# Stage one of a hybrid encoder: input fed by columns, row sums from matmuls, a fixed order of the first round

## The chip, the cores and the metric

The kernel runs on one core of a Trainium2 chip. The metric is the time of one execution on the device in microseconds (us); a profiled execution also leaves a trace of what each engine did. Engines are named as in the profile: PE (TensorE), DVE (VectorE), ACT (ScalarE), POOL (GpSimd) and SP (SyncE, which here only issues DMAs).

## The reference

One encoder layer is computed for two request groups that share all weights: a sample of 2048 tokens and a prompt of 512 tokens, each 1024 wide.

```
mod = silu(c) @ w_ada + b_ada            # shift, scale, gate_res: one row per group
h = rms_norm(x, g_norm) * (1 + scale) + shift
proj = h @ w_in                          # qa ka va za | cq ckv kr zb | gm
ya = windowed_gqa(qa, ka, va, sink) * silu(za)
yb = mla(cq, ckv, kr, g_q, w_uq, g_kv, w_ukv) * silu(zb)
ga, gb = split(sigmoid(gm))
x + gate_res * ((ga * (ya @ w_oa) + gb * (yb @ w_ob)) @ w_out)   # then a final rms_norm
```

`rms_norm` divides each row (token) by the root of the mean of its squares. The change touches how `h` is made from `x`.

## The kernel before

Everything is float32. A product in full precision is made of three matmuls on a high and a low part of each operand (`mm3`, L99 to L102): the high part is the value rounded by a copy on ACT, the low part is what the rounding left, from a subtraction on DVE (activations) or POOL (weights, L122 and L123).

The 2560 tokens go in five chunks of 512, four of the sample and one of the prompt. Three stages follow each other. Stage one (up to about 520 us) makes `h` and every projection that the latent attention needs. Stage two (to about 1640 us) is the latent attention, in an order written by hand. Stage three makes the gates, the windowed attention and the output.

In stage one the projections want `h` with the 1024 columns on the partitions, in eight tiles of 128 columns by 512 tokens. The input lies by rows. `load_x` (L233) loads four tiles of 128 rows, sums the squares of each row on ACT (L240), raises the mean to the power -1/2 on POOL (L97) and scales the rows on DVE (L242). `x_cols` (L249) turns them: four PE transposes of 128x128 for each of the eight tiles into a PSUM bank (L252). `h_tile` (L255) then makes `h32 = a*x + b` on DVE (L258) and the high part `hh` on ACT (L261), both from the bank and beside each other, and the low part on DVE (L262); `h32` goes to DRAM (`h_d`, L263), where stages two and three fetch it again (`load_h`, L637 and L638).

The columns `a` and `b` (`acol`, `bcol`) come from the modulation, in the block from L516, in four groups of 256 columns: matmuls `pm` (L561) on weights `wa` that stream in, four small copies into `mod` by DVE and ACT in turn (L568, L570), two small matmuls `pc` (L573), and five small DVE steps (L577 to L581). Round a of chunk 0 (`tka`, L100 to L102) multiplies `h` tile by tile into four PSUM banks, one for each 128 tokens, so it follows the four groups. After it come `ka` (one bank, 24 matmuls), round b (`tkb`) and four `qa`, with the tiles of the next chunk made between the `qa`. `norm_c` (L428) ends a bank: a sum of squares on ACT (L432), then a copy to `cn` and a scaling on DVE (L434, L435).

PSUM has four banks for accumulation here, so `ka` can start only when the first bank of round a has been read out. Each engine works through its own queue in order. A scheduler sets that order from its own estimate of times; only stage two is written by hand. Loads of the chunks' weights are issued by ACT, those of input by SP, whose queue they share with the stores of results.

## Time and profile before

| | us |
|---|---|
| median of 3 runs | 2647.18 |
| lowest and highest | 2646.66 and 2648.54 |
| profiled execution | 2646.29 |
| its span, first to last instruction | 2644.5 |
| PE busy in the span | 2563.1 (97%) |
| POOL busy | 1599.2 |
| DVE busy | 1698.1 |
| ACT busy | 1326.4 |

The mean granted clock of TensorE is 0.992 of full speed. A busy engine counts from the start to the end of its instructions, and neighbouring matmuls overlap, so the cost of one is read from the distance of the starts.

### The profile page before, as it was taken

What the parts mean: (1) busy time and instruction counts of PE and PEld (TensorE: products, weight loads), DVE (VectorE), ACT (ScalarE), POOL (GpSimd) and SP (SyncE); (2) the same over time, 40 slices, a digit from 0 to 9 for tenths busy, and PEclk for the clock granted to TensorE, in tenths of its full rate; (3) what the DMA queues carried; (4) which work ended last, traced back from release to release, by engine and by line L of the source; (5) the groups of instructions that cost most, each with busy time, mean ns of one, the idle gap of its engine ahead of it and who ended that gap; (6) DMA issues with size and microseconds to landing.
All of it is one profiled execution on the core that took longest, in us unless ns stands there. A gap on an engine that the chain in (4) does not pass through costs nothing. (4 is left out here: it accounts for less than half of the span.)

```text
span 2644.5 us, 33977 instructions
## 1 busy us (share of the span) xinstructions
PE 2563.1 (97%) x11842; PEld 2036.0 (77%) x11842; DVE 1698.1 (64%) x2511; ACT 1326.4 (50%) x2105; POOL 1599.2 (60%) x992
## 2 busy tenths in 40 slices
PE   6999999899999999999999999999999999999998
PEld 4888888677777777776777777877887788778876
DVE  4654644579999999999864566436644664466325
ACT  3554543267777777777644443434343444344432
POOL 2564554278888888887852376337733773377355
PEclk9999999999999999999999999999999999999999
DMA  8677765563132222212264545344544453445341
GB/s 308 215 241 239 243 208 187 153 185 94 54 95 75 67 79 74 81 58 82 84 218 150 162 167 191 122 148 173 189 133 144 164 193 121 161 152 200 102 172 50
DMA packets 199432, 392.34 MB, mean 148 GB/s; under 512 B 18087, under 2 KB 97384, under 8 KB 197659
## 3 DMA queue, kind: packets, MB, share of 16 engines
q1 hardware_dynamic: 186210, 353.32, 41.3%
q10 hardware_dynamic: 13050, 36.86, 4.3%
q8 instruction: 93, 1.52, 0.2%
q14 instruction: 79, 0.64, 0.1%
HBM read 286.52 MB, written 103.58 MB: 148 GB/s over the span
## 5 line engine op out<-in xcount | busy, mean ns | idle before, releaser
L735 POOL TENSOR_TENSOR pl<-pf,ph 128x1024 fp32r<-128x1024 f32 x272 | 655.6, 2413 | 137.5 <-ACT pf L728 133.9
L123 POOL TENSOR_TENSOR wlgm<-wrgm,whgm 128x1024 fp32r<-128x1024 f32 x80 | 196.5, 2460 | 328.2 <-ACT whgm L122 291.0
L727 ACT ACTIVATE ph<-s 128x1024 fp32r<-128x1024 f32 x272 | 278.7, 1025 | 183.9 <-PE s L720 182.7
L686 DVE TENSOR_REDUCE mx<-mp 128x1 f32<-128x1024 f32 x240 | 292.7, 1220 | 39.0 <-PE mp L680 36.5
L748 DVE TENSOR_TENSOR ac<-ac,pf 128x512 f32<-128x512 f32 x424 | 294.2, 694 | 16.5 <-ACT pf L728 9.6
L728 ACT ACTIVATE pf<-s 128x1024 f32<-128x1024 f32 x272 | 275.8, 1014 | 0.0
L101 PE MATMUL gm<-H,wlgm 128*128 128x512 f32 x640 | 252.3, 395 | 0.0
L100 PE MATMUL gm<-H,whgm 128*128 128x512 f32 x640 | 250.3, 395 | 0.9 <-ACT whgm L122 0.9
L102 PE MATMUL gm<-H,whgm 128*128 128x512 f32 x640 | 251.0, 394 | 0.0
L718 PE MATMUL s<-Q,K 97*128 97x512 f32 x544 | 216.7, 398 | 3.9 <-DMA Q<-qr_d 3.9
L719 PE MATMUL s<-Q,K 96*128 96x512 f32 x544 | 216.9, 399 | 0.0
L720 PE MATMUL s<-Q,K 96*128 96x512 f32 x544 | 215.5, 396 | 0.0
L760 PE MATMUL a<-ph,V 128*128 128x512 f32 x544 | 175.3, 403 | 0.0
L763 PE MATMUL a<-pl,V 128*64 128x512 f32 x544 | 170.7, 395 | 0.9 <-POOL pl L735 0.8
L680 PE MATMUL mp<-K,Q 96*128 96x512 f32 x512 | 162.4, 398 | 5.8 <-DVE mx L686 3.7
L123 POOL TENSOR_TENSOR wlz<-wrz,whz 128x1024 fp32r<-128x1024 f32 x39 | 94.2, 2424 | 120.5 <-ACT whz L122 118.0
L167 DVE CUSTOM_DVE_ANT_0 S<-as,mask,snk 128x384 f32<-128x384 f32 (+1 forms) x160 | 89.2, 585 | 99.2 <-PE as L165 66.9
L188 DVE TENSOR_TENSOR PT<-pT,PT 128x512 fp32r<-128x512 f32 x112 | 77.1, 688 | 108.9 <-ACT PT L187 107.4
L100 PEld LDWEIGHTS gm<-H,whgm 128*128 128x128 f32 x640 | 119.4, 188 | 26.4 <-issue 1.7
L102 PEld LDWEIGHTS gm<-H,whgm 128*128 128x128 f32 x640 | 120.3, 188 | 23.8
L101 PEld LDWEIGHTS gm<-H,wlgm 128*128 128x128 f32 x640 | 120.3, 188 | 23.8
L100 PE MATMUL z<-H,whz 128*128 128x512 f32 x320 | 127.2, 398 | 9.2 <-ACT whz L122 4.8
(254 smaller groups left out, 6501.2 us busy)
## 6 DMA issues: line engine op xcount, KB each, us to landing
wrgm<-in_t_col_dram SPq DMA_DIRECT2D x80, 512.0 KB
wrz<-in_t_col_dram SPq DMA_DIRECT2D x40, 512.0 KB
wrw<-in_t_out_dram SPq DMA_DIRECT2D x40, 512.0 KB
wrqa<-in_t_col_dram ACTq DMA_DIRECT2D x20, 512.0 KB
qa_d<-qa SPq DMA_DIRECT2D x40, 256.0 KB
k_d<-kn SPq DMA_DIRECT2D x20, 512.0 KB
qn_d<-qn SPq DMA_DIRECT2D x20, 512.0 KB
v_d<-vt SPq DMA_DIRECT2D x20, 512.0 KB
```

Source lines behind the costliest of these rows:

```text
L100: nc.tensor.matmul(ps, wh, mh, start=first, stop=False)
L101: nc.tensor.matmul(ps, wl, mh, start=False, stop=False)
L102: nc.tensor.matmul(ps, wh, ml, start=False, stop=last)
L123: (eng or nc.gpsimd).tensor_tensor(out=wl[:, :n], in0=wr[:, :n], in1=f(wh[:, :n]), op=ALU.subtract)
L686: nc.vector.tensor_reduce(out=it.mx[:, i // 2, i % 2:i % 2 + 1], in_=it.mp.rearrange("p a b -> p (a b)"), axis=AX.X, op=ALU.max)
L718: nc.tensor.matmul(ps[:, j, :], K[0:97, 0, ks], Q[0:97, 0, :], start=True, stop=False)
L719: nc.tensor.matmul(ps[:, j, :], K[0:96, 1, ks], Q[0:96, 0, :], start=False, stop=False)
L720: nc.tensor.matmul(ps[:, j, :], K[0:96, 0, ks], Q[0:96, 1, :], start=False, stop=True)
L727: nc.scalar.activation(ph, it.s, AF.Exp)
L728: nc.scalar.activation(pf, it.s, AF.Exp)
L735: nc.gpsimd.tensor_tensor(out=pl, in0=it.pf[p], in1=f(it.ph[p]), op=ALU.subtract)
L748: nc.vector.tensor_tensor(out=sm if last and j else it.acc, in0=it.acc, in1=pf[:, j], op=ALU.add)
```

## The change

The host lays out a copy of the input by columns, in a new DRAM tensor `t_x`. Each chunk loads it with four DMAs of 512 KB (`xT`). The rows are no longer turned. For chunks 1 to 4 the rows are still loaded, but only to sum their squares. `spread` turns the four columns of row factors into one tile `R` in which every partition holds the factors of the 512 tokens: four transposes of a broadcast column, and one ACT copy. Chunk 0 does not load rows at all: `first_x` squares the column tiles on ACT and DVE and sums them over partitions with 32 matmuls against a column of ones.

`h_tile` now makes `h32 = xT*a*R` on DVE, then `hh = h32 + b` on ACT, which follows the DVE step, then the low part on DVE. The tile stored in DRAM lacks `b`, and `load_h` adds it. In `norm_c` the sum of squares writes into `cn` itself, so the DVE copy into `cn` follows it.

In chunk 0, the order on PE is written out: the first modulation group, the spread, and then for each pair of tiles the round's matmuls, with the next modulation group between the two. All weights of round a are loaded by SP between the modulation's weights.

```diff
+        def spread(c, rss):
+            pt = px(tt(c, 0), f"pt{c}")
+            for t in range(4):
+                nc.tensor.transpose(pt[:, t * P:(t + 1) * P], rss[t].broadcast_to([P, P]), ident)
+            R = tl("R", [P, T], F32, f"R{c}", 1)
+            nc.scalar.copy(R, pt)
+            return R
...
-                nc.scalar.activation(jk, xt, AF.Square, accum_out=ss)
+                nc.scalar.activation(xt, xt, AF.Square, accum_out=ss)
                 rstd(rs, ss, D, p1, f"x{c}_{t}", "rvx")
-                nc.vector.tensor_scalar(out=xt, in0=xt, scalar1=rs, scalar2=None, op0=ALU.mult)
-                xts.append(xt)
-            return xts
+                rss.append(rs)
+            return load_xT(c), spread(c, rss)
...
+        def first_x(tp):
...
+                if k % 2:
+                    nc.vector.tensor_tensor(out=sq[:, 1], in0=x, in1=x, op=ALU.mult)
+                else:
+                    nc.scalar.activation(sq[:, 0], x, AF.Square)
+                for t in range(4):
+                    nc.tensor.matmul(pss[t][:, 0:1], sq[:, k % 2, t * P:(t + 1) * P], one, start=(k == 0),
+                                     stop=(k == KD - 1))
...
-            nc.vector.tensor_scalar(out=h32, in0=src, scalar1=acol[:, g, k:k + 1], scalar2=bcol[:, g, k:k + 1],
-                                    op0=ALU.mult, op1=ALU.add)
...
-            nc.scalar.activation(hh[:, 0, :], src, AF.Identity, bias=bcol[:, g, k:k + 1], scale=acol[:, g, k:k + 1])
-            nc.vector.tensor_tensor(out=hh[:, 1, :], in0=h32, in1=f(hh[:, 0, :]), op=ALU.subtract)
+            nc.vector.scalar_tensor_tensor(out=h32, in0=xts[k // 2][:, k % 2], scalar=a, in1=R, op0=ALU.mult,
+                                           op1=ALU.mult)
+            nc.scalar.activation(hh[:, 0, :], h32, AF.Identity, bias=b)
+            nc.vector.scalar_tensor_tensor(out=hh[:, 1, :], in0=h32, scalar=b, in1=f(hh[:, 0, :]), op0=ALU.add,
+                                           op1=ALU.subtract)
...
-                nc.scalar.activation(jk[:, 0:n], ps, AF.Square, accum_out=ss)
+                nc.scalar.activation(dst, ps, AF.Square, accum_out=ss)
...
+            with tc.manual_schedule(engines={nc.tensor.engine}):
+                mod_mm(0)
+                wa_load(3)
+                src0 = src0[0], spread(0, src0[1])
+                mod_fin(0)
+                pss0 = [pa(f"tka0_{t}") for t in range(4)]
+                for q in range(4):
+                    a_mm(2 * q, range(4))
+                    if q == 0:
+                        a_load(3)
+                    if q < 3:
+                        mod_mm(q + 1)
+                        a_split(q + 1)
+                    a_mm(2 * q + 1, range(2))
+                    if q < 3:
+                        mod_fin(q + 1)
+                    a_mm(2 * q + 1, range(2, 4))
...
-        nc.scalar.copy(hh[:, 0, :], hr)
-        nc.vector.tensor_tensor(out=hh[:, 1, :], in0=hr, in1=f(hh[:, 0, :]), op=ALU.subtract)
+        b = bcol[:, c // NS, k:k + 1]
+        nc.scalar.activation(hh[:, 0, :], hr, AF.Identity, bias=b)
+        nc.vector.scalar_tensor_tensor(out=hh[:, 1, :], in0=hr, scalar=b, in1=f(hh[:, 0, :]), op0=ALU.add,
+                                       op1=ALU.subtract)
```

Where PE stands at the end of chunk 0's round a, before: the last of its matmuls (`tka0_3`, on the eighth tile `hh0_7`), and `ka0` behind it.

```order
L101 MATMUL tka0_3_498<-wha0_6_587,hh0_7_474 128x512
L102 MATMUL tka0_3_498<-wla0_6_588,hh0_7_474 128x512
L100 MATMUL ka0_661<-hh0_0_320,whka0_664 128x512
L101 MATMUL ka0_661<-hh0_0_320,wlka0_665 128x512
L102 MATMUL ka0_661<-hh0_0_320,whka0_664 128x512
```

The same place after: three of the four transposes of chunk 1's row factors (`rs1_0` to `rs1_2`) stand between the two.

```order
L101 MATMUL tka0_3_346<-wha0_6_520,hh0_7_545 128x512
L102 MATMUL tka0_3_346<-wla0_6_521,hh0_7_545 128x512
L243 MATMUL pt1_718<-ident_60,rs1_0_681 128x128
L243 MATMUL pt1_718<-ident_60,rs1_1_689 128x128
L243 MATMUL pt1_718<-ident_60,rs1_2_697 128x128
L100 MATMUL ka0_640<-hh0_0_333,whka0_643 128x512
L101 MATMUL ka0_640<-hh0_0_333,wlka0_644 128x512
L102 MATMUL ka0_640<-hh0_0_333,whka0_643 128x512
```

What moved: `ka0` now has three instructions ahead of it that wait for the rows of chunk 1.

SP's queue at that time, before: the stores of chunk 0's `h` (`h_d0`) and the loads of the rows of chunk 1 (`x1`).

```order
L263 DMA h_d0_0_70<-h2_0_318 128x512 x2
L263 DMA h_d0_1_71<-h2_1_369 128x512 x2
L263 DMA h_d0_2_72<-h2_2_418 128x512 x2
L236 DMA x1_0_699<-in_x_sample_dram 128x1024
L236 DMA x1_1_709<-in_x_sample_dram 128x1024
L263 DMA h_d0_3_73<-h2_3_467 128x512 x2
L236 DMA x1_2_719<-in_x_sample_dram 128x1024
L236 DMA x1_3_729<-in_x_sample_dram 128x1024
```

The same after, with chunk 1's columns (`xT1`) behind the rows.

```order
L298 DMA h_d0_0_70<-h2_0_332 128x512 x2
L298 DMA h_d0_1_71<-h2_1_401 128x512 x2
L298 DMA h_d0_2_72<-h2_2_470 128x512 x2
L298 DMA h_d0_3_73<-h2_3_539 128x512 x2
L252 DMA x1_0_678<-in_x_sample_dram 128x1024
L252 DMA x1_1_686<-in_x_sample_dram 128x1024
L252 DMA x1_2_694<-in_x_sample_dram 128x1024
L252 DMA x1_3_702<-in_x_sample_dram 128x1024
L236 DMA xT1_0_710<-in_t_x_dram 128x1024
L236 DMA xT1_1_712<-in_t_x_dram 128x1024
L236 DMA xT1_2_714<-in_t_x_dram 128x1024
L236 DMA xT1_3_716<-in_t_x_dram 128x1024
```

What moved: all stores of chunk 0's `h` stand ahead of the first row load.

PE between the third and the fourth `qa` of chunk 0, before: eight transposes (`pt1_4` and `pt1_5`) of chunk 1's rows.

```order
L101 MATMUL qa0_2_1087<-hh0_7_474,wlqa0_2_1091 128x512
L102 MATMUL qa0_2_1087<-hh0_7_474,whqa0_2_1090 128x512
L252 MATMUL pt1_4_1125<-ident_60,x1_0_699 128x128
L252 MATMUL pt1_4_1125<-ident_60,x1_1_709 128x128
L252 MATMUL pt1_4_1125<-ident_60,x1_2_719 128x128
L252 MATMUL pt1_4_1125<-ident_60,x1_3_729 128x128
L252 MATMUL pt1_5_1136<-ident_60,x1_0_699 128x128
L252 MATMUL pt1_5_1136<-ident_60,x1_1_709 128x128
L252 MATMUL pt1_5_1136<-ident_60,x1_2_719 128x128
L252 MATMUL pt1_5_1136<-ident_60,x1_3_729 128x128
L100 MATMUL qa0_3_1147<-hh0_0_320,whqa0_3_1150 128x512
L101 MATMUL qa0_3_1147<-hh0_0_320,wlqa0_3_1151 128x512
```

The same place after.

```order
L101 MATMUL qa0_2_1049<-hh0_7_545,wlqa0_2_1053 128x512
L102 MATMUL qa0_2_1049<-hh0_7_545,whqa0_2_1052 128x512
L101 MATMUL qa0_3_1099<-hh0_0_333,wlqa0_3_1103 128x512
L102 MATMUL qa0_3_1099<-hh0_0_333,whqa0_3_1102 128x512
L100 MATMUL qa0_3_1099<-hh0_1_338,whqa0_3_1102 128x512
```

What moved: the transposes are gone, and nothing took their place; the transposes of the other six tiles are gone in the same way.

## Rows read from the trace of the kernel before

**Rows 1.** Windows of 66 us: from:to, length, busy us per engine, PEclk, DMA, GB/s

```profile
132.20:198.30 66.10, 66.03 (x362) 57.04 (x361) 38.54 (x69) 35.47 (x74) 43.44 (x70) 1.00 0.76 241
...
330.50:396.60 66.10, 66.10 (x362) 57.47 (x362) 31.54 (x56) 27.07 (x57) 34.64 (x53) 1.00 0.66 208
396.60:420.00 23.40, 21.25 (x104) 16.98 (x103) 8.56 (x13) 8.35 (x16) 6.78 (x12) 0.93 0.33 93
```

**Rows 2.** Timeline, TensorE in chunk 2: start, length us, line, work

```profile
275.69 0.39 PE L102 MATMUL qa<-hh,whqa 128*128 128x512 f32 x1
275.91 0.39 PE L100 MATMUL qa<-hh,whqa 128*128 128x512 f32 x1
276.14 0.60 PE L252 MATMUL pt<-ident,x 128*128 128x128 f32 x4
276.50 0.48 PE L101 MATMUL qa<-hh,wlqa 128*128 128x512 f32 x1
276.81 0.40 PE L102 MATMUL qa<-hh,whqa 128*128 128x512 f32 x1
277.05 0.40 PE L100 MATMUL qa<-hh,whqa 128*128 128x512 f32 x1
```

**Rows 3.** Windows of 10 us while the first projection round runs

```profile
40.00:50.00 10.00, 8.33 (x55) 5.55 (x54) 4.63 (x13) 4.80 (x8) 4.69 (x2) 0.83 0.40 119
50.00:60.00 10.00, 7.15 (x27) 5.48 (x27) 4.56 (x12) 2.43 (x3) 2.10 (x2) 0.78 0.60 206
```

**Rows 4.** Timeline, TensorE in chunk 0, waits in brackets

```profile
26.47 1.19 PE L100 MATMUL tka<-wha,hh 128*128 128x512 f32 x4 [2.84 <-ACT hh L261]
...
41.19 1.48 PE L561 MATMUL pm<-wa,cols 128*2 128x256 f32 x24
42.60 0.61 PE L573 MATMUL pc<-fold,mod 98*128 98x4 f32 x4
...
58.13 0.63 PE L101 MATMUL tka<-wha,hh 128*128 128x512 f32 x1
...
64.04 0.39 PE L102 MATMUL tka<-wla,hh 128*128 128x512 f32 x1
65.09 0.47 PE L100 MATMUL ka<-hh,whka 128*128 128x512 f32 x1 [0.67 <-DVE cn L434]
```

**Rows 5.** Timeline, all engines, copies of the modulation sums

```profile
39.28 0.41 DVE L570 COPY mod<-pm 2x256 f32<-2x256 f32 x1 [3.17 <-PE pm L561]
...
40.59 0.37 ACT L568 COPY mod<-pm 2x256 f32<-2x256 f32 x1 [0.49 <-DVE mod L570]
```

**Rows 6.** Timeline, VectorE of chunk 0, third and fourth modulation group

```profile
44.85 0.98 DVE L258 TENSOR_SCALAR h<-xT,acol,bcol 128x512 f32<-128x512 f32 x2
...
53.09 0.16 DVE L577 TENSOR_TENSOR bcol<-pc,cols 128x2 f32<-128x2 f32 x1 [5.61 <-PE pc L573]
...
53.57 2.77 DVE L258 TENSOR_SCALAR h<-xT,acol,bcol 128x512 f32<-128x512 f32 x2
```

**Rows 7.** Timeline, GpSimd beside it

```profile
53.56 2.04 POOL L123 TENSOR_TENSOR wlb<-wrb,whb 128x864 fp32r<-128x864 f32 x1 [3.50 <-ACT whb L122]
```

**Rows 8.** Groups of VectorE instructions by shape, 60 to 530 us

```profile
L262 DVE TENSOR_TENSOR hh<-h,hh 128x512 fp32r<-128x512 f32 x32 | 35.5, 1113 | 4.8 <-ACT hh L261 4.2
...
L434 DVE COPY cn<-tka 128x384 f32<-128x384 f32 x20 | 10.8, 546 | 0.0
```

**Rows 9.** Groups of ScalarE instructions by shape, 60 to 530 us

```profile
L261 ACT ACTIVATE hh<-pt,bcol,acol 128x512 fp32r<-128x512 f32 x32 | 24.7, 780 | 17.7 <-DVE h L258 17.5
...
L240 ACT ACTIVATE jx<-x 128x1024 bf16<-128x1024 f32 x16 | 16.8, 1053 | 3.2 <-POOL wla L123 3.1
...
L432 ACT ACTIVATE jkcq<-tka 128x384 bf16<-128x384 f32 x20 | 10.0, 499 | 1.6 <-DVE v_cq L96 1.2
```

**Rows 10.** One line, ScalarE reading the hidden tiles back, stages 2 and 3

```profile
L637 ACT CAST H<-hr x40: 603/618/622, 1193.8 to 2362.9; 128x512 fp32r<-128x512 f32 x40
```

**Rows 11.** One line, VectorE on the same tiles: ns min/median/max

```profile
L638 DVE TENSOR_TENSOR H<-hr,H x40: 678/692/2900, 1196.9 to 2363.6; 128x512 fp32r<-128x512 f32 x40
```

More of the change, by code (lines that the diff above doesn't have):

```diff
@@ L230, in rope, with load_xT @@
             nc.gpsimd.tensor_tensor(out=dst[:, :, hi], in0=dst[:, :, hi], in1=tmp[:, :nh, hi], op=ALU.add)
+        def load_xT(c):
+            out = []
+            for k2 in range(KD // 2):
+                xt = tl("hh", [P, 2, T], F32, f"xT{c}_{k2}", NH)
+                nc.sync.dma_start(xt.rearrange("p k n -> p (k n)"), t_x[c, k2])
+                out.append(xt)
+            return out
+        def spread(c, rss):
[5 more added lines that the diff above has]
+            return R
         def load_x(c):
-            xts = []
+            rss = []
             for t in range(4):
@@ L446, in tail_a @@
                 norm_c(t, ps[:, 128:512], 384, cns[t][:, 0:384], "cq")
-            round_("a", [(0, 2), (2, 2), (4, 2), (6, 2)], 512, t_a, tail_a)
+            if c:
+                round_("a", [(0, 2), (2, 2), (4, 2), (6, 2)], 512, t_a, tail_a)
+            else:
+                for t in range(4):
+                    tail_a(t, env["pss0"][t])
             if c == NC - 1:
@@ L487, in chunk @@
                 if nxt is not None:
-                    nH += [h_tile(nxt, k, x_cols(nxts, nxt, k)) for k in (2 * j, 2 * j + 1)]
+                    nH += [h_tile(nxt, k, nxts) for k in (2 * j, 2 * j + 1)]
             C = []
@@ L534, in encoder @@
             sc = cols[:, 0:16].rearrange("p (g k) -> p k g", g=2)
-            XT = []
-            for k in range(KD):
-                if k % 2 == 0:
-                    xt2 = tl("hh", [P, 2, T], F32, f"xT{k}", NH)
-                pt = x_cols(xts, 0, k)
-                if k % 2:
-                    nc.scalar.copy(xt2[:, 1], pt)
-                else:
-                    nc.vector.tensor_copy(xt2[:, 0], pt)
-                XT.append(xt2[:, k % 2])
+            src0 = first_x(p0)
             H = []
@@ L560, in encoder @@
                             r = 32 * (2 * i + n)
[L561 to L564 removed]
+                            nc.tensor.matmul(pm[r:r + 2, 0:256], sc[:, k + i, :], was[q, k][:, i, n, :],
+                                             start=(k == 0), stop=(k == KD - 2))
                 for i in range(4):
@@ L1100 @@
     feeds += list(_tables().items())
+    feeds.append(("t_x", _columns(inputs["x_sample"], inputs["x_prompt"])))
     for name, a in feeds:
```

66 lines of the change are left out of this document (47 added, 19 removed).

## The prediction

> **What bounds the kernel now.** I read the windows first, because a busy share over the whole span hides that the stages differ. From 66 to 396 us PE has no idle time to speak of: the window from 132.2 is busy for 66.03 of 66.10 us, the one from 330.5 for all of it, and the three others between 66 and 396 us look the same; the granted clock is 1.00 [rows 1]. DVE, ACT and POOL are busy for half to two thirds of these windows, and the DMA engines for 0.66 to 0.76. What leaves PE's queue there shortens the run one for one; what is added to another engine is hidden as long as nothing is handed to PE later than now. Two stretches are different. From 396.6 to 420 us PE is busy for 21.25 of 23.40 us at a clock of 0.93 [rows 1]: the last tiles of `h` for the fifth chunk are made there, and PE waits for them. And in the first 65 us a chain runs from engine to engine, round a starting at 26.47 us and ending at 64.43 [rows 4], with the clock at 0.83 and 0.78 in the windows from 40 and from 50 [rows 3]. Stage two keeps its hand-written order, and stage three's matmuls stay the same ones.
>
> **Transposes, chunks 1 to 4.** Of 128 transposes 16 remain (the spread), so 112 go. Their price is a distance, not a duration: from the matmul that starts at 275.91 to the one at 277.05 there lie 1.14 us, for three matmul distances and four transposes. Matmuls start 0.22 to 0.24 apart beside it, 0.23 in the mean, so four transposes cost 1.14 - 0.69 = 0.45, and one 0.113 [rows 2]. 112 x 0.113 = 12.7 us. The DVE scaling of the rows goes too, and the tile's DVE step now reads SBUF in place of a bank: both off PE's path.
>
> **The end of chunk 3.** There the new `h` tiles need no PE and no bank of their own. Only `R` and the loaded columns are needed, both there long before. PE's 2.15 us of idle time in that window should go, and part of the loss to the clock (0.07 x 23.4 = 1.6). I take 3.0; nothing is the other end.
>
> **Chunk 0, until `ka`.** The written order makes the round a period. It begins with 12 matmuls, 12 x 0.227 = 2.7 us (the distance in [rows 2]); then comes a modulation group: 32 matmul records, 24 of which took 1.48, so 2.0 in all [rows 4]. Then PE depends on a chain: the four copies into `mod`, from 39.28 to 40.59 + 0.37, 1.7 us [rows 5]; `pc`, 0.6 [rows 4]; the column steps, from 53.09 to 53.57, 0.5 [rows 6]; two `h32` steps and one low part on DVE, 3 x 0.69, priced by a DVE step with the same two SBUF inputs [rows 11]. The sum is 4.9, with hand-overs 5.0. The remaining 12 matmuls and `pc` lie in that chain's shadow. Period: 2.7 + 2.0 + 5.0 = 9.7 us. The first matmul of the round started at 26.47. The row factors now have to pass the spread and a copy, while eight transposed copies go; I put its start at 27.5. The round would end at 27.5 + 3 x 9.7 + 2 x 2.7 = 62.0 us. To that I add 2.5 for what the ideal chain leaves out: part of the time at half clock (matmuls 0.43 apart, as from 58.13 on, where one lasts 0.63 instead of 0.39 [rows 4]), and POOL beside DVE (below). So the round ends at 64.5, about where it did.
>
> Behind it `ka` now waits longer. Before, it started 0.66 us after the end, once a bank had been read out [rows 4]. In the queue now three transposes of chunk 1's row factors stand ahead of it, and the third row tile is squared on ACT only after the copies of the finished banks, ahead of the square that frees the first bank; the copy to `cn` follows that square instead of running beside it. That is a square of 1.05, a square of 0.50 [rows 9], a copy of 0.55 [rows 8], and about 0.8 for accumulator reads, `va` and hand-overs: 2.9 us. Chunk 1's rows are also loaded later, behind all stores of chunk 0; their DMAs are issued at about 55 us, so the third tile should lie there shortly before 62 and is not what comes last, though closely. `ka` starts at 64.5 + 2.9 = 67.4 instead of 65.09: a loss of 2.3 us. The ends are a gain of 2.4 (62.0 + 0.7) and a loss of 25 (the third rival).
>
> **Stages two and three.** Reading `h` back costs ACT an addition with a bias column instead of a cast. The nearest rows are 0.780 for such a step (from a bank) against 0.618 [rows 9, 10]. Forty times 0.16 is 6.5 us on ACT, hidden under matmuls except for the first tiles of a chunk, where PE waits for the first: two for each of five chunks, 1.6 us. If none is hidden it is 6.5; nothing is the other end. The DVE step keeps its two inputs. The later release of a bank in `norm_c`, 40 times up to 0.55 [rows 8], lies beside other banks' matmuls; I count 1.0 for all, between nothing and 5. The order of stage three also shifts a little in the queues. No row prices that; it can go either way, and I leave it at nothing, plus or minus 3.
>
> **Sum.** -12.7 - 3.0 + 2.3 + 1.6 + 1.0 = -10.8 us against the profiled execution's 2646.29 us, that is 2635.5; the median lies 0.9 above it, so I say 2636.4. The DMA traffic grows by 2 MB a chunk, against some 16 MB in each 66 us (241 GB/s [rows 1]); with a share of 0.76 there is room, and I count nothing. If an in-order queue holds a store behind such a load, a bank comes free later.
>
> **Rivals.**
>
> First, the early stretch gains too. In its favour: in the old order round a shared PE with the tail of the modulation as the scheduler happened to put it, and two of its four weight loads waited in ACT's queue. Then the round ends at 62.0, `ka` starts at 62.7 (-2.4), and the small charges vanish: -12.7 - 3.0 - 2.4 = -18.1, or 2629. Against it: the chain per group has become longer, since ACT's high part now follows DVE.
>
> Second, DVE and POOL get in each other's way, and the gain is mostly lost. A pair of `h32` steps took 0.98 us at 44.85 and 2.77 at 53.57, when a POOL subtraction of 2.04 us started at 53.56 [rows 6, 7]; and the low parts, which read two SBUF tiles, took 1.113 us each in stage one [rows 8] against 0.692 in the median later [rows 11]. Such a meeting costs 1.8 us on the chain. Every group has two pairs (`h32` and the low parts), so eight in chunk 0; if half of them meet a weight split on POOL, that is 7.2 us, and the time becomes -10.8 + 7.2 = -3.6, or 2643.6, which a measurement can hardly tell from no change (about 0.2%, 5 us). Against it: there are only four such splits in the round, and part of the 2.5 us above is this already. The Trainium skill, "SBUF — State Buffer" (Who interferes with whom), says that a DVE instruction with two SBUF inputs contends with a POOL instruction that reads SBUF, and that the later one waits until the other is done. By that rule the new `h32`, which reads `xT` and `R`, contends in every chunk, where the old one read a bank. [...] In chunks 1 to 4 it would fall on engines with a third of their time free.
>
> Third, slower: half clock throughout round a. The new order puts a gap of some 2 us into each period: the chain of 5.0 less the 2.7 + 0.6 of work beside it. PE's clock has been seen to fall after such gaps: after `pc` at 42.60 PE ran dry, and the window from 40 has 0.83 [rows 3, 4]. At half clock the period would be 5.4 + 4.0 + 6.0 (then the 12 matmuls and `pc` are longer than the chain), 15.4 us, and the round would end at 27.5 + 46.2 + 10.8 = 84.5, 20 us later, with `ka` 5 us longer. The total is -10.8 + 25 = +14, or 2661. It decides once more than two thirds of the stretch from 27 to 65 us run at half clock (two thirds: +5.9, or 2653). Against it: the old order had gaps of 2.84 us and the like, and its windows were still at 0.78 and more.
>
> **How the numbers follow.** The forecast, 2636, holds with 0.52; its own range is 2630 to 2642. The first rival has 0.15, the second 0.20, the third 0.13. Faster: the forecast without its upper edge (0.50), the first rival and a small part of the second, 0.67. Slower: the third, where it is severe, 0.12. The same: 0.21. The range from 2626 to 2651 takes in the first two rivals and the mild half of the third.
>
> **What would show it.** Right: PE still without idle time from about 70 us on, with the stretch up to the last `qa` of chunk 3 about 13 us shorter; no wait of the kind in the window at 396.6; `ka` of chunk 0 starting at 65 to 69 us, preceded by a wait of 2 to 3 us; a period of 9 to 11 us between the `pc` matmuls. Wrong: idle time of PE in chunks 1 to 4, for a tile, a bank or a weight; `h32` steps of 2 us in chunk 0; windows at 0.6 or less before 65 us; stage two or three longer by more than 5 us.

## The result, and the profile after

The change makes the kernel slower by about 22 us (by the ratio). The forecast was 2636.4, and the range ended at 2651.

| | before | after |
|---|---|---|
| median of 4 runs, us | 2646.92 | 2669.84 |
| lowest and highest, us | 2643.57, 2648.54 | 2664.04, 2670.70 |
| ratio to before, 95% interval | | 1.0083 [1.0071, 1.0095] |
| span of the profiled execution, us | 2644.5 | 2668.9 |

The page of the kernel after, its first lines (span, then busy time, share and instructions of each engine):

```profile
span 2668.9 us, 33774 instructions
PE 2576.4 (97%) x11766; PEld 2043.7 (77%) x11766; DVE 1673.4 (63%) x2492; ACT 1324.3 (50%) x2102; POOL 1603.8 (60%) x989
```

PE is busy 13 us longer than before, though 112 transposes are gone, and it idles some 11 us more: where it waits and where its clock is low has to be asked stage by stage. For that I follow the starts of a few matmuls through the program. The last columns are the differences, and what each stretch added.

| start, us | before | after | difference | added |
|---|---|---|---|---|
| first `tka`, chunk 0 | 26.5 | 31.4 | +4.9 | +4.9 |
| first `ka`, chunk 0 | 65.1 | 83.9 | +18.8 | +13.9 |
| first `qa`, chunk 0 | 85.0 | 107.0 | +22.0 | +3.2 |
| first `s` (stage two) | 529.2 | 536.5 | +7.3 | -14.7 |
| last `mp` (stage two) | 1285.0 | 1302.3 | +17.3 | +10.0 |
| last `out` (stage three) | 2636.0 | 2660.3 | +24.3 | +7.0 |

The stretch of chunks 1 to 4, from the first `qa` to the first `s`, thus gains about what was forecast. Everything else loses. The last stretch, which I call stage three below, starts at the last `mp` and so takes in the end of stage two. The windows of the kernel after, in the columns of [rows 1], show the gain's place:

```profile
66.10:132.20 66.10, 57.40 (x303) 47.52 (x292) 45.10 (x81) 36.75 (x75) 35.95 (x46) 0.95 0.74 257
132.20:198.30 66.10, 65.12 (x352) 56.08 (x351) 30.65 (x56) 31.79 (x64) 35.63 (x41) 1.00 0.80 269
330.50:396.60 66.10, 66.10 (x355) 57.60 (x354) 39.16 (x63) 31.20 (x65) 40.54 (x59) 1.00 0.77 258
396.60:420.00 23.40, 23.40 (x117) 19.69 (x116) 6.50 (x10) 8.84 (x15) 11.45 (x10) 1.00 0.64 183
```

The window from 396.6 is now full, at a clock of 1.00, where it had 21.25 at 0.93. The one from 66 is not: chunk 0 is late, and it is that window's 8.7 us of idle time which a reader of the whole page would miss.

TensorE of the kernel after, from the start to the first `tka`; it answers to the first line of [rows 4]:

```profile
8.39 7.41 PE L274 MATMUL ss<-one,sq 128*128 128x1 f32 x34 [8.39 <-ACT sq L272]
...
16.00 6.56 PE L274 MATMUL ss<-one,sq 128*128 128x1 f32 x30
22.49 3.59 PE L597 MATMUL pm<-wa,cols 128*2 128x256 f32 x32
28.20 1.02 PE L609 MATMUL pc<-fold,mod 98*128 98x4 f32 x4 [1.06 <-ACT mod L602]
31.36 0.80 PE L100 MATMUL tka<-wha,hh 128*128 128x512 f32 x1 [2.15 <-ACT hh L295]
```

The 32 matmuls against a column of ones are 64 records (34 and 30, with one small transpose between), and hold PE from 8.4 to 22.5 us without a gap. The modulation stands behind them in PE's order.

Windows of 10 us after: that of the squares, and four of the round, which answer to [rows 3]:

```profile
10.00:20.00 10.00, 10.00 (x48) 9.89 (x47) 0.41 (x3) 1.06 (x2) 2.35 (x1) 1.00 1.01 385
...
40.00:50.00 10.00, 6.55 (x21) 4.83 (x22) 4.92 (x10) 2.28 (x3) 2.35 (x1) 0.77 0.29 98
50.00:60.00 10.00, 7.64 (x52) 3.83 (x50) 3.87 (x11) 3.01 (x5) 1.68 (x1) 0.89 0.15 54
60.00:70.00 10.00, 8.54 (x54) 5.27 (x55) 2.83 (x6) 0.73 (x2) 0.67 (x1) 0.83 0.11 29
70.00:80.00 10.00, 7.02 (x23) 5.08 (x22) 4.90 (x14) 4.52 (x8) 2.76 (x3) 0.83 0.81 294
```

From 40 us on PE is busy 6.5 to 8.5 of 10 us, part of it at the lower of its two clocks, and VectorE, ScalarE and GpSimd are busy for 4.9 at most: a chain that hands on from engine to engine. One period of it, all engines, in the kernel after (matmuls in between left out):

```profile
41.05 1.41 DVE L293 SCALAR_TENSOR_TENSOR h<-xT,acol,R 128x512 f32<-128x512 f32 x2
...
41.83 1.04 ACT L122 CAST wha<-wra 128x1024 fp32r<-128x1024 f32 x1 [1.95 <-PE tka L101]
...
42.78 1.33 ACT L295 ACTIVATE hh<-h,bcol 128x512 fp32r<-128x512 f32 x2
43.00 2.35 POOL L123 TENSOR_TENSOR wla<-wra,wha 128x1024 fp32r<-128x1024 f32 x1 [7.66 <-ACT wha L122]
43.53 3.04 DVE L296 SCALAR_TENSOR_TENSOR hh<-h,bcol,hh 128x512 fp32r<-128x512 f32 x2 [1.07 <-ACT hh L295]
...
45.96 0.80 PE L101 MATMUL tka<-wha,hh 128*128 128x512 f32 x1 [1.92 <-DVE hh L296]
```

The first `h32` tile is there about 41.75, but ACT casts the next weight first, and that cast itself had waited for PE. The high parts start 0.95 late. The cast also starts POOL's subtraction at 43.00, half a microsecond ahead of DVE's two low parts, and these take 3.04 us. The periods begin at 31.36, 43.55, 58.87 and 72.72: they last 12.2, 15.3 and 13.9 us, and the last 24 matmuls 9.1.

### The profile page after: what moved, and what is told of

It is laid out like the page before. It is cut to its first block, busy times and chain, and to the rows that moved or that the text cites. A ratio compares the mean times of both kernels' runs of the same rounds, so it can differ in the third digit from the quotient of the medians.

```text
span 2668.9 us, 33774 instructions
## 1 busy us (share of the span) xinstructions
PE 2576.4 (97%) x11766; PEld 2043.7 (77%) x11766; DVE 1673.4 (63%) x2492; ACT 1324.3 (50%) x2102; POOL 1603.8 (60%) x989
## 5 line engine op out<-in xcount | busy, mean ns | idle before, releaser
L749 PE MATMUL mp<-K,Q 96*128 96x512 f32 x512 | 163.8, 401 | 10.8 <-DVE mx L755 8.2
L1015 DVE SCALAR_TENSOR_TENSOR G<-G,po 128x512 f32<-128x512 f32 x80 | 53.5, 682 | 137.2 <-PE po L102 100.9
```

## The experiments

My theory after the comparison: chunk 0's loss comes from PE's written order, through three things in it (the squares' matmuls at the start, the cast ahead of the high parts, and POOL beside DVE); stage two's from single DVE steps that now start just behind a POOL instruction; stage three's from the order in which the scheduler places its work. The rivals: the loss is the new data path itself (`xT`, `R`, the serial chain through ACT), in all chunks; or the bias added on reading back; or one delay from chunk 0 that is only carried on. All times are us, in the table as in the one above; a ratio is against the kernel before on the same chip.

| kernel | first `ka` | first `qa` | first `s` | first to last `mp` | last `mp` to last `out` | median | ratio |
|---|---|---|---|---|---|---|---|
| before | 65.1 | 85.0 | 529.2 | 738.8 | 1351.0 | | |
| after | 83.9 | 107.0 | 536.5 | 747.8 | 1358.0 | 2669.84 | 1.0083 [1.0071, 1.0095] |
| chunk0_old | 64.9 | 90.5 | 521.1 | 742.5 | 1353.9 | 2644.60 | 0.9988 [0.9978, 0.9998] |
| loadh_old | 82.8 | 106.4 | 537.2 | 744.3 | 1360.9 | 2669.15 | 1.0081 [1.0057, 1.0105] |
| cast_late | 73.1 | 98.0 | 527.6 | 748.0 | 1360.6 | 2664.68 | 1.0064 [1.0040, 1.0088] |
| presum | 72.1 | 95.1 | 524.8 | 747.3 | 1362.8 | 2663.99 | 1.0061 [1.0038, 1.0085] |
| no_pool | 69.0 | 96.6 | 527.6 | 746.3 | 1354.9 | 2657.63 | 1.0036 [1.0024, 1.0048] |
| norm_old | 64.9 | 87.6 | 517.8 | 743.1 | 1358.5 | 2649.38 | 1.0003 [0.9993, 1.0014] |
| bestold | 65.6 | 86.4 | 521.5 | 741.2 | 1370.0 | 2656.01 | 1.0033 [1.0022, 1.0043] |
| allnew | 60.3 | 80.9 | 515.5 | 743.2 | 1357.9 | 2646.51 | 0.9999 [0.9989, 1.0008] |
| fixed_off | 68.1 | 93.5 | 524.3 | 746.3 | 1356.3 | 2652.02 | 1.0017 [1.0005, 1.0028] |
| c0order | 65.6 | 90.9 | 526.7 | 742.7 | 1354.1 | 2652.20 | 1.0022 [1.0012, 1.0033] |
| neworder | 62.4 | 88.0 | 524.5 | 742.9 | 1355.5 | 2646.76 | 0.9995 [0.9986, 1.0004] |
| neworder_late | 61.0 | 86.8 | 523.5 | 738.7 | 1352.5 | 2645.14 | 0.9991 [0.9982, 0.9999] |
| full3 | 61.8 | 82.5 | 518.2 | 738.6 | 1354.2 | 2639.03 | 0.9968 [0.9956, 0.9979] |
| full2 | 60.6 | 81.2 | 516.9 | 739.0 | 1352.9 | 2637.44 | 0.9961 [0.9947, 0.9974] |

**chunk0_old**: chunk 0 as before (rows, transposes, the scheduler's order), chunks 1 to 4 as changed.

```diff
+            xts = load_x0(0)
-            src0 = first_x(p0)
...
-            with tc.manual_schedule(engines={nc.tensor.engine}):
...
+                    H.append(h_tile0(0, k, XT[k], h2[:, k % 2]))
```

> Chunk 0 alone as in the kernel before (rows loaded and transposed, order of round a left to the scheduler); chunks 1 to 4 and the read-back of h for them are the new ones. Theory: the loss sits in chunk 0 (ka starts 18.8 us late there) and in the end of stage two, while chunks 1 to 4 gain about 12 to 16 us. Then ka starts at 65 to 69 us, the first matmul of stage two's scores at 514 to 520 us (529.2 before, 536.5 after), and the time is 2632 to 2645. Rival: the new tiles of chunks 1 to 4 cost as much as the transposes saved (DVE against POOL, DMA); then the scores start at 527 to 535 and the time is 2647 to 2660.

`ka` is back where it was, and the run is 25 us faster than the change's. From the first `qa` to the first `s` it takes 430.6 us, where the kernel before takes 444.2 and the change 429.5: the gain of chunks 1 to 4 does not depend on chunk 0, and the data path by columns is not what loses there. That rival falls. But of 13.6 gained only about 3 reach the time (ratio 0.9988): the first `qa` waits, and stages two and three are longer here too, so the loss is not one delay of chunk 0 carried on, either. In TensorE of chunk0_old:

```profile
83.83 0.60 PE L558 MATMUL ct<-ident,cn 128*128 128x128 f32 x4
90.52 0.76 PE L100 MATMUL qa<-hh,whqa 128*128 128x512 f32 x1 [6.09 <-DVE v_ckv L96]
```

PE stands still for 6.1 us until a bank has been read out. VectorE and ScalarE of the same run show what that reading out waits for:

```profile
82.80 2.41 DVE L329 SCALAR_TENSOR_TENSOR hh<-h,bcol,hh 128x512 fp32r<-128x512 f32 x1 [0.81 <-ACT hh L328]
...
87.21 0.38 ACT L497 ACTIVATE cn<-tkb 128x256 f32<-128x256 f32 x1
87.25 2.73 DVE L655 SCALAR_TENSOR_TENSOR wkl<-wkr,cols,wkh 128x512 fp32r<-128x512 f32 x4
...
89.96 0.41 DVE L499 COPY cn<-tkb 128x256 f32<-128x256 f32 x1
```

And VectorE in the kernel before:

```profile
78.08 4.88 DVE L590 SCALAR_TENSOR_TENSOR wkl<-wkr,cols,wkh 128x512 fp32r<-128x512 f32 x4
...
83.05 0.41 DVE L434 COPY cn<-tkb 128x256 f32<-128x256 f32 x1
```

The copy `cn` that frees the first bank of round b starts 2.4 us after the square of that bank is done (87.59), because VectorE first makes steps for chunk 1's tiles (`hh`) and the low parts of the up-projection's weights (`wkl`). In the kernel before none of chunk 1's steps stand ahead of this copy, and it is done at 83.46, while PE ends round b at 83.55. The 16 transposes that stood there (1.91 us at 83.39) covered no wait.

**loadh_old**: the added bias on reading back is left out.

```diff
-        nc.scalar.activation(hh[:, 0, :], hr, AF.Identity, bias=b)
+        nc.scalar.copy(hh[:, 0, :], hr)
```

> The changed kernel with the read-back of h in stages two and three as before (a cast and a subtraction; the addition of the bias column b is left out). Theory: the 9 us that stage two loses between its first and last mp matmul come from the longer DVE step meeting POOL's subtractions (2.92 us instead of 0.68 in one place, then a DVE weight split of 3.40 instead of 1.21), so from first to last mp it takes 739 us again (738.8 before, 747.8 after), and the time is about 2658 to 2663. Rival: the loss there is a matter of when stage two starts against the transfers and of the order of its queues, not of the read-back; then it stays at 745 to 749 and the time at 2667 to 2671.

Stage two gets 3.5 us shorter, not 9, and nothing is left of it at the end (ratio 1.0081 against 1.0083). The read-back is a part of stage two's loss and not its main one. By its own rows a read-back on ACT now takes 0.717 us in the median, against 0.618 [rows 10].

**cast_late**: the next weight's cast follows the high parts, with ACT's order written out too.

```diff
+            a_split(1)
-            with tc.manual_schedule(engines={nc.tensor.engine}):
+            with tc.manual_schedule(engines={nc.tensor.engine, nc.scalar.engine}):
...
-                        a_split(q + 1)
...
                     a_mm(2 * q + 1, range(2, 4))
+                    if q < 2:
+                        a_split(q + 2)
```

> The changed kernel with the order of ScalarE in round a of chunk 0 written out too: the weight casts of round a follow the high parts of h instead of standing ahead of them. Theory: in each period the cast delays the high part by 1.0 us, and POOL's subtraction that it releases holds the low part on DVE for 1.6 to 1.9 us more; the gaps bring PE to half clock. Then in the second and third period the two low parts take about 1.4 us together instead of 3.04, the periods shrink from 15.3 and 13.9 us to 10 to 12, ka starts at 74 to 79 instead of 83.9, and the time is 2658 to 2665. Rival: the period is set by the chain of copies, columns and three DVE steps in any order; then periods stay above 13 us and ka starts at 82 to 85.

The same stretch in cast_late, all engines:

```profile
41.98 1.38 ACT L295 ACTIVATE hh<-h,bcol 128x512 fp32r<-128x512 f32 x2 [1.95 <-DVE h L293]
...
42.73 1.41 DVE L296 SCALAR_TENSOR_TENSOR hh<-h,bcol,hh 128x512 fp32r<-128x512 f32 x2
42.75 0.19 PEld L100 LDWEIGHTS tka<-wha,hh 128*128 128x128 f32 x1 [1.00 <-ACT hh L295]
...
43.27 1.04 ACT L122 CAST wha<-wra 128x1024 fp32r<-128x1024 f32 x1
...
44.38 2.39 POOL L123 TENSOR_TENSOR wla<-wra,wha 128x1024 fp32r<-128x1024 f32 x1 [18.25 <-ACT wha L122]
```

The low parts take 1.41 us in place of 3.04, since POOL starts behind them. The second period is 9.9 us (42.75 to 52.62) in place of 15.3, and the clock 1.00 from 40 to 60 us. The third, where a cast for round b still stands ahead of the high parts, is 10.7; the first is still 12.2, with its first matmuls at the lower clock. `ka` starts 10.8 us sooner. Cast and POOL moved together here, so this run gives the price of both.

**presum**: the squares are added up on DVE first, so that 4 matmuls remain of 32.

```diff
-                for t in range(4):
-                    nc.tensor.matmul(pss[t][:, 0:1], sq[:, k % 2, t * P:(t + 1) * P], one, start=(k == 0),
-                                     stop=(k == KD - 1))
+                if k:
+                    nc.vector.tensor_tensor(out=sq[:, k % 2], in0=acc, in1=sq[:, k % 2], op=ALU.add)
+                acc = sq[:, k % 2]
+            for t in range(4):
+                nc.tensor.matmul(pss[t][:, 0:1], acc[:, t * P:(t + 1) * P], one, start=True, stop=True)
```

> The changed kernel with the squares of chunk 0 added over the eight column tiles on DVE first, so that 4 matmuls against the column of ones remain of 32. Theory: the 32 took PE from 9.7 to 22.6 us and held the first modulation group back, which starts at 22.5 instead of 14.9. With 4 the modulation group starts at 14 to 17 us and the first matmul of round a at 26 to 28.5 instead of 31.4; ka starts 3 to 5 us earlier. Rival: the start of round a is set by the loads and the weight casts on ScalarE; then it stays at 30 to 31.4.

TensorE of presum at the start:

```profile
12.79 2.74 PE L597 MATMUL pm<-wa,cols 128*2 128x256 f32 x24 [2.29 <-DVE cols L568]
15.47 1.87 PE L275 MATMUL ss<-one,sq 128*128 128x1 f32 x8
...
24.03 0.79 PE L100 MATMUL tka<-wha,hh 128*128 128x512 f32 x1 [2.13 <-ACT hh L295]
```

The modulation starts 9.7 us sooner and the first `tka` 7.3; `ka` gains 11.8. The matmuls at the start are a cause of their own. The rest of the 11.8 comes from the second period, which lasts 10.8 in place of 15.3: the cast does not stand ahead of the high parts there, though that order was not written out.

**no_pool**: the low parts of the weights of round a, `ka` and the first of round b are left out in chunk 0, so that POOL stands still beside DVE.

```diff
+        if nm in ("a0_0", "a0_2", "a0_4", "a0_6", "ka0", "b0_0"):
+            return wh, wh
```

> The changed kernel without POOL's subtractions for the weights of round a, of ka and of the first part of round b in chunk 0 (their low parts are left out, the high part stands in for them); the weight casts still stand ahead of the high parts on ScalarE. Theory: the cast and the meeting of DVE and POOL cost separately. Without POOL the two low parts take 1.4 us together in every group instead of 3.0, while the high part still waits 1.0 us for the cast; the last three periods (15.3, 13.9 and about 14 us) shrink by 1.6 us and whatever part of the half clock goes with it, to 10.5 to 13, and ka starts at 74 to 80 instead of 83.9. Rival: the low parts wait for ScalarE and not for POOL; then they still take 2.5 to 3 us, and ka starts at 82 to 84.

A low part takes 0.75 us, the second period is 9.9, and `ka` starts at 69.0. The cast (at 41.75) also came to stand between the two high parts here, since PE freed its tile sooner, so this run doesn't tell the two apart either; the undisturbed chain is the same 9.9 as in cast_late.

**norm_old**: chunk0_old, with the scratch tile for the squares back in `norm_c`, so that its copy to `cn` need not follow the square (and two buffers for `h32` in place of three).

```diff
-                nc.scalar.activation(dst, ps, AF.Square, accum_out=ss)
+                jk = p1a.tile([P, D], BF16, name=f"jk{nm}{c}_{t}", tag="junkx", bufs=1)
+                nc.scalar.activation(jk[:, 0:n], ps, AF.Square, accum_out=ss)
```

> The kernel with chunk 0 as before, and with the sum of squares of norm_c written to a scratch tile again, so that the copy to cn need not follow it (to make room, the h32 tiles have two buffers instead of three). Theory: PE's wait of 6.1 us before the first qa of chunk 0 comes from banks that are read out later, and 1.7 us of transposes that used to stand there no longer cover it. Then that wait shrinks to 1 to 3.5 us, the first qa starts at 85.5 to 88 instead of 90.5, the scores of stage two start at 516 to 519.5 instead of 521.1, and the time falls by 2 to 5 us, to 2639 to 2643. Rival: the wait has another cause (squares of chunk 1's rows or up-projection weights ahead in the queues of ScalarE and DVE); then it stays above 4.5 us and the time within 2 us of 2644.6.

The first `qa` comes 2.9 us sooner and `s` 3.3, but PE still waits 3.59 us there. The rows do not put this gain down to `norm_c`: in chunk0_old the copy did not wait for the square. What changed on VectorE ahead of the first copy is the work for chunk 1's tiles, six steps of 6.6 us in chunk0_old and four of 3.0 here, two tiles in place of three, as the buffers for `h32`. At the end nothing of the gain is left: stage three is 4.6 longer than in chunk0_old, and the ratio 1.0003.

**bestold** and **allnew**: `h` is stored with its bias again, so that stages two and three have the very operations of the kernel before (the stored tile is a second ACT step, off the chain), the spread follows the first `qa`, and `norm_c` is as before. bestold has the old chunk 0; allnew the new one, with presum's squares and cast_late's order, and the splits of the next weights written out as well.

```diff
+            xt = xts[k // 2][:, k % 2]
+            nc.vector.scalar_tensor_tensor(out=xt, in0=xt, scalar=a, in1=R, op0=ALU.mult, op1=ALU.mult)
...
+            nc.scalar.activation(h32, xt, AF.Identity, bias=b)
...
+                    if j == 0:
+                        nxts = nxts[0], spread(nxt, nxts[1])
```

> As the kernel before this one, and h is stored with b again by one more ScalarE step a tile, so that the read-back in stages two and three is that of the kernel before; the spread of a chunk's row factors stands behind the first qa in the program. Theory: the 32 more ScalarE steps (0.78 us each, 25 us in 330) are hidden, so the scores of stage two start at 515 to 520, and the place in stage two where the longer read-back met POOL (2.9 us) is as before; the time is 2632 to 2642. Rival: ScalarE becomes late in chunks 1 to 4; the scores start at 522 or later.

> The changed scheme with what the runs point to: squares of chunk 0 added on DVE before 4 matmuls, ScalarE's order in round a written out with each weight cast behind the high parts (round b's first too), norm_c and the stored h as before the change. Theory: the first matmul of round a starts at 23 to 26 us, the periods are 9.7 to 10.5 us, ka starts at 60 to 66 (65.1 before, 83.9 after); with the saving of chunks 1 to 4 the scores of stage two start at 510 to 518, and the time is 2626 to 2640. Rival: half clock or the loads keep ka at 68 or later, and the time at 2640 or more.

allnew's `ka` starts at 60.3 us, 4.8 sooner than before the change, and `s` 13.7 sooner: stage one does all that was hoped of it. The last `mp` is still 9.1 ahead, the last `out` only 2.2. bestold loses even more, 19 us in stage three. Since these stages have the operations of the kernel before, operations can't be the cause. What differs is their order: in after, loadh_old, cast_late, presum, norm_old, bestold and allnew the scheduler's order of stage three on PE differs from that of before (in after 2267 of 6024 records are other ones, place by place), and with it that on VectorE and ScalarE; in the other eight it is the same on PE, row for row. The seven with another order need 1357.9 to 1370.0 us from the last `mp` to the last `out`, the others 1352.5 to 1356.3. That an order of the same operations goes with up to 19 us more than that of before (1351.0) is as far as this goes. It is not the whole loss either: allnew and norm_old keep the order of before on PE for the first 2201 records, some 495 us, and have lost 3.3 and 3.4 us by then, as much as neworder and fixed_off, which keep it to the end (3.6 and 3.4). I have read in the traces that PE waits longer for the windowed attention's `PT` (7.1 us in all in after, 4.5 before), but have not changed that by itself.

**fixed_off**: the change with the scheduler's order on PE in chunk 0 in place of the written one.

```diff
-            with tc.manual_schedule(engines={nc.tensor.engine}):
+            if True:
```

> The changed kernel with the order of PE in round a of chunk 0 left to the scheduler again. Theory: the written order runs each modulation group just ahead of the tiles that need it, so that copies, columns, h32, high and low part all lie on the path in each period; the scheduler lets a group run ahead. Then periods are 9 to 12 us, ka starts at 69 to 76 instead of 83.9; stage three has PE's instructions in the order of the kernel before again and takes 1353 to 1356 us from the last mp matmul to the last out matmul (1351.0 before, 1358.0 after), and the time is 2650 to 2660. Rival: the written order costs nothing by itself; then ka stays at 80 to 84 and the time at 2663 or more.

`ka` at 68.1 in place of 83.9, and the ratio falls from 1.0083 to 1.0017: some 17 us of 22 are gone. The written order, as it stood on PE alone, is the largest single cause. The scheduler orders the same operations without it.

**c0order**, **neworder** and **neworder_late**: with a bias in the stored tile, the pool sizes were chosen so that stage three keeps the order of before. c0order has the old chunk 0, neworder the new one of allnew (with the early spread). neworder_late also moves one weight split of stage two (`wlz`, on DVE) a step later.

```diff
-        NH, WB = 20, 12
+        NH, WB = 19, 12
...
-        at(230 + 2 * KD, "h", lambda: W0.append(w_cols(p3r, "z0_1_0", C_ZB, NR, [(p3r, 1)], nc.vector)))
+        at(231 + 2 * KD, "h", lambda: W0.append(w_cols(p3r, "z0_1_0", C_ZB, NR, [(p3r, 1)], nc.vector)))
```

> Chunk 0 as before, chunks 1 to 4 new, h stored with b by one more ScalarE step a tile; norm_c as in the change. The order of PE in stage three is that of the kernel before. Theory: stage three costs what its order costs, whatever stage one does. Then from the last mp to the last out matmul it takes 1353 to 1356 us (the kernel bestold, with another order there and the same operations, took 1370.0), the scores start at 519 to 523, and the time is 2640 to 2646. Rival: the extra ScalarE steps or the state of the queues at the end of stage two make stage three longer; then it takes 1358 or more and the time is 2648 or more.

> As allnew, but with the spread where the change has it, three h32 buffers and 19 instead of 20 buffers for the input tiles; by this the order of PE in stage three is that of the kernel before. Theory: allnew's gain of 13.7 us at the start of the scores was given back in two places, by one weight split on DVE near the end of stage two that just misses POOL (3.7 us), and by stage three's order (7 us). Here stage three takes 1353 to 1356 us (1357.9 in allnew), and the time is 2636 to 2643. Rival: the order is not the cause; stage three takes 1357 to 1360 again and the time is 2644 to 2649.

> As the kernel neworder, with the DVE weight split near the end of stage two one unit later (behind two additions instead of behind the one that POOL has just held up). Theory: that split takes 1.2 us again instead of 3.4, and from first to last mp stage two takes 738 to 740 us instead of 743; the time is 3 to 4 us under neworder's. Rival: the place meets POOL in the same way or the loss has another cause; then it stays at 742 or more.

Stage three is short in all of them; c0order and bestold have the same operations there, and need 1354.1 and 1370.0. The times of c0order and neworder still miss what was expected. In c0order `s` comes 5.6 us later than in chunk0_old: the second ACT step a tile is not free there. In neworder `s` comes 9.0 later than in allnew. Stage two is 742.7 to 742.9 with the split where it was, and 738.7 with it moved: 4.2 us from one step's place. The medians of neworder and neworder_late differ by 1.6 us only, which their intervals don't tell apart, so the 4.2 rests on the traces. VectorE and GpSimd around this split, in the kernel before:

```profile
1248.16 1.21 DVE L123 TENSOR_TENSOR wlz<-wrz,whz 128x1024 fp32r<-128x1024 f32 x1
1248.37 5.60 POOL L735 TENSOR_TENSOR pl<-pf,ph 128x1024 fp32r<-128x1024 f32 x2 [0.68 <-ACT pf L728]
```

In the kernel after:

```profile
1261.56 2.41 POOL L804 TENSOR_TENSOR pl<-pf,ph 128x1024 fp32r<-128x1024 f32 x1 [0.38 <-ACT pf L797]
1261.66 3.40 DVE L123 TENSOR_TENSOR wlz<-wrz,whz 128x1024 fp32r<-128x1024 f32 x1
```

In neworder_late:

```profile
1245.83 1.22 DVE L123 TENSOR_TENSOR wlz<-wrz,whz 128x1024 fp32r<-128x1024 f32 x1
...
1246.55 5.10 POOL L824 TENSOR_TENSOR pl<-pf,ph 128x1024 fp32r<-128x1024 f32 x2 [0.82 <-ACT pf L817]
```

Where DVE starts first its step takes 1.21, and where POOL is 0.1 us ahead, 3.40. PE then waits for the maximum behind it (3.09 us in chunk0_old, which has the same two starts 0.10 apart), and the matmuls behind that wait start 0.43 apart. The read-back has its own meeting. In the kernel before:

```profile
1224.14 0.68 DVE L638 TENSOR_TENSOR H<-hr,H 128x512 fp32r<-128x512 f32 x1
1224.15 2.92 POOL L735 TENSOR_TENSOR pl<-pf,ph 128x1024 fp32r<-128x1024 f32 x1 [0.48 <-ACT pf L728]
```

And after:

```profile
1234.14 2.38 POOL L804 TENSOR_TENSOR pl<-pf,ph 128x1024 fp32r<-128x1024 f32 x1 [0.47 <-ACT pf L797]
1234.15 2.92 DVE L706 SCALAR_TENSOR_TENSOR H<-hr,bcol,H 128x512 fp32r<-128x512 f32 x1
```

One hundredth of a microsecond ahead or behind decides which of the two waits. DVE loses this meeting in every kernel that adds the bias when it reads chunk 0 back, and in none of the others. Over all sixteen kernels stage two falls into three groups: 738.6 to 739.0 us where DVE loses neither meeting (before, neworder_late, full3 and full2), 741.2 to 744.3 where it loses that of the split, and 746.3 to 748.0 where it loses both. The Trainium skill, "SBUF — State Buffer" (Who interferes with whom), has the rule: a DVE instruction with two SBUF inputs and a POOL instruction that reads SBUF exclude each other, and the order of issue decides who waits. These rows agree with it: in the kernel after, the DVE steps of 2.92 and 3.40 us end 0.55 and 1.09 us after POOL's, a little less than they take where they start first.

**full3** and **full2**: allnew with the split moved and the order of stage three as before; three and two buffers for `h32`. What was open: whether a gain in stage one reaches the end at all, once these two are out of the way.

> allnew's stage one (the spread behind the first qa) with three h32 buffers and 19 input tiles, the weight split near the end of stage two one unit later, and PE's order in stage three as in the kernel before. Theory: the three parts add up. Stage two's scores start at 514 to 518 us, first to last mp takes 738 to 740, last mp to last out 1352 to 1356; so the last out starts at 2622 to 2630 (2636.0 before) and the time is 2633 to 2641. Rival: a gain in stage one is given back later in any case, since stages two and three are bound by loads or by other engines; then the last out is at 2632 or later and the time at 2643 or more.

> The same with two h32 buffers, as in allnew. Theory: as for the kernel before; the scores start at 514 to 517. The two differ by less than 3 us. Rival: as above.

It does. full2 reaches `s` 12.3 us sooner than the kernel before, and the last `out` 9.5. It beats both kernels: 2637.44 against 2646.43 on the same chip. full3 and neworder_late differ in the place of the spread alone, and `s` comes 5.3 us sooner where the spread follows the first `qa`. PE's wait before the first `qa` is 0.95 us in place of 6.67: ahead of the first copy `cn` of round b, VectorE has no step of chunk 1's tiles in full3, and twelve (9.0 us) in neworder_late. This edit alone shows what that wait is made of. Round a of full2, on TensorE:

```profile
22.03 0.80 PE L100 MATMUL tka<-wha,hh 128*128 128x512 f32 x1 [2.27 <-ACT hh L297]
...
33.55 0.50 PE L100 MATMUL tka<-wha,hh 128*128 128x512 f32 x1 [0.59 <-ACT hh L297]
...
43.49 0.49 PE L100 MATMUL tka<-wha,hh 128*128 128x512 f32 x1 [0.61 <-ACT hh L297]
...
53.38 0.50 PE L100 MATMUL tka<-wha,hh 128*128 128x512 f32 x1 [0.59 <-ACT hh L297]
...
60.59 0.47 PE L100 MATMUL ka<-hh,whka 128*128 128x512 f32 x1 [0.69 <-DVE cn L475]
```

Its periods are 11.5, 9.9 and 9.9 us, the first with matmuls at the lower clock until 26 us, and the waits for a high part 0.6.

## Why the prediction was wrong

**What held.** The transposes and the end of chunk 3 were to give 12.7 and 3.0 us. Of the 128 transposes, 16 lie ahead of chunk 0's first `qa`; without them 112 x 0.113 less 1.8 is 10.9, and with 3.0 it is 13.9. From the first `qa` to the first `s` the change measures 14.7. The signs that were named for it are there: PE without idle time in the window from 330 us, and none at 396.6.

**The step that failed: "Chunk 0, until `ka`".** It says +2.3; it is +18.8. It had three parts:

- "I put its start at 27.5": it was 31.4. The sum named the spread and a copy, and gave no price to the 32 matmuls against a column of ones, which were in the diff. With 4 of them it is 24.0.
- "Period: 9.7 us". The chain was rightly priced: 9.9 in cast_late, no_pool and full2. But the change writes out PE's order and leaves ACT's to the scheduler, which puts the weight cast ahead of the high parts. I hadn't read ACT's queue there; the chain took for granted that ACT is free.
- "To that I add 2.5 for what the ideal chain leaves out". It came to 14.6.

These 14.6 us can be read from the starts of the matmuls, each stretch of the kernel after against the undisturbed one (the second period of cast_late, the last stretch of full2):

| us more than undisturbed | period 1 | 2 | 3 | last 24 matmuls | sum |
|---|---|---|---|---|---|
| from the first matmul behind `pm` to the next period (cast ahead of the high parts) | 0.9 | 1.0 | 0.8 | | 2.7 |
| first to second matmul (low parts beside POOL) | | 1.6 | 1.6 | 1.3 | 4.5 |
| the matmuls after it (lower clock) | 1.4 | 2.9 | 1.6 | 1.6 | 7.4 |

For the second period: from 43.55 to 45.96, to 53.38 and to 58.87 there lie 2.41, 7.42 and 5.49; in cast_late 0.79, 4.55 and 4.53. With the late start (3.9), the chain itself (9.9 for 9.7, and 6.1 for 5.4 at the end, 1.3 in all), less the 2.5 and 0.8 that the step below had too much, that is 3.9 + 1.3 + 14.6 - 3.3 = 16.5, from 67.4 to 83.9.

"Behind it `ka` now waits longer", 2.9: the round ended at 81.77 and `ka` starts at 83.87, 2.1 us, of which PE waits 1.31 for the row factors. That was nearly right.

**`norm_c`, 1.0, and the work on VectorE.** No run shows the later release by itself; at chunk 0's first `qa` the copy has long been free to start when it does. What the sum put at nothing is the work for chunk 1's tiles on VectorE. These tiles no longer wait for transposes, and the scheduler places six of their steps (6.5 us in after) ahead of the copies that free round b's banks, where there was none before. PE waits 4.14 us there in after, and from `ka` to the first `qa` it takes some 3 us longer. The prediction had named the condition, that such work is hidden "as long as nothing is handed to PE later than now"; it did not hold here.

**Reading `h` back, 1.6, and stage two "keeps its hand-written order".** Its order did stay; it lost 9.0 us and 1.0 ahead of it. The ACT step I priced (0.16 more) is 0.10 more, and hidden. What I left out is DVE beside POOL: two steps that now start behind a POOL instruction rather than ahead of it. Of the 9.0, the moved split explains 4.2 and the read-back's bias 3.5; the means of the three groups (738.8, 742.8 and 747.1) put the two at 4.0 and 4.3. The rest, about 1, stays open, and so does why the split starts behind POOL even in kernels whose stage two is that of before.

**Stage three, "plus or minus 3".** It is +7.0, and from +1.5 to +19 over all the runs. What goes with the longer times is the order, on PE, VectorE and ScalarE at once; no run changes the order on one engine alone. A term of plus or minus 3 had no room for an order that costs unchanged operations 19 us (bestold). Why a change in stage one gives another order there isn't settled.

**The rivals.** The second named the right mechanism, DVE beside POOL, with 7.2 us in chunk 0: it was 4.5 there, and another 8 or so in stage two, where it wasn't looked for. Its pair of 2.77 us (53.57) was not a step with two such inputs: in chunk 0 the old `h32` step read one tile in SBUF, `xT`, and not a bank, so the case for the new step rested on the low parts. The third, half clock all through round a, would have given 2661 or more. The windows show 0.77 to 0.89, not that, but the lower clock is the largest of the three rows above. It goes with the gaps: behind the waits of 1.53 and 1.92 us (43.55 and 45.96) the matmuls start 0.43 apart, and in cast_late's second period, with waits of 0.57 and 0.29, nearly all of them 0.23. Not every gap does it: in the kernel before, the matmuls behind the wait of 2.84 us at 26.47 start 0.23 apart. (Behind `pc` at 42.60, which the prediction took for the place where PE ran dry, eight `pm` still ran; the wait of 1.67 came after them.) So the forecast had both rivals' mechanisms in view and took each for a small one; it lacked what brings them on together, the cast in ACT's queue.

**The clear-cut part.** fixed_off shows some 17 of the 22 us to be the written order. What is left there is what stages two (+7.5) and three (+5.3) and the first `qa` lose, less the gain of chunks 1 to 4. The parts don't add up exactly, since an edit in stage one can change the order of stage three, too.

## What to carry to other kernels

Where one engine's order is written out and the others' is left to a scheduler, read the queues of the others at the critical place: one weight cast ahead of the chain's step cost 1 us a period there, POOL's start behind it 1.6, and the lower clock after both waits up to 2.9. Before you count work on another engine as hidden, look at what stands behind it in that engine's queue: here steps for the next tiles held back the copies that free PE's banks. And before you count a gain in one stage, follow a few starts to the end: here 13.6 us became 3. Price every added instruction in the diff, the small ones too.

## What the runs showed of the hardware that was not expected

A matmul with a single float32 column on the moving side is no cheaper than a product of 512 columns here: 32 of them left 64 records, which held PE for 13.8 us, 0.215 each, against 0.23 for a record of 512 columns. From 10 to 20 us the weight loads were busy for 9.89 of 10.00 us. In stage two a shift of 0.02 to 0.3 us against POOL decides whether a DVE step with two SBUF inputs takes 0.68 or 2.92 us, and 1.21 or 3.40. Stage three, with unchanged operations, ran in 1351.0 to 1370.0 us.
